# Hybrid encoder step: wide decay rows of the Mixer in three sets of two, loaded one use ahead

## The chip, the cores and the metric

One core of a Trainium2 chip. The metric is the device time of one execution in microseconds. A core has TensorE (PE, matmuls), VectorE (DVE), ScalarE (ACT), GpSimd (POOL) and SyncE (SP). Each engine works through its own instructions in the order in which they were written to it, and an instruction that waits holds those behind it on the same engine. DMA transfers are issued from SP, ACT and POOL; an issue stands in its engine's order like any other instruction.

## The reference

One layer over 512 prompt frames and 64 sample frames (576 columns in the kernel): half a SwiGLU, a Mixer, half a SwiGLU, a norm. The Mixer projects its input once and runs three branches: a Mamba-2 scan in 4 groups of 4 heads (`ssd`), band attention in 8 heads (`attn`), and 4 matrix memories (`ml`). What the change touches are the decays. For the scan, with `cum` the running sum of the log decays over the frames:

```python
cum = jnp.cumsum(dtc * a, axis=1)
seg = cum[:, :, None] - cum[:, None, :]
lmat = jnp.exp(jnp.where(causal, seg, -jnp.inf))
w = cb[..., None] * lmat * dtc[:, None]
y = jnp.einsum('btsgr,bsgrp->btgrp', w, xc)
y = y + jnp.exp(cum)[..., None] * jnp.einsum('btgn,bgrpn->btgrp', cc, h)
wd = jnp.exp(last[:, None] - cum) * dtc
h = jnp.exp(last)[..., None, None] * h + jnp.einsum('bsgr,bsgn,bsgrp->bgrpn', wd, bc, xc)
```

The matrix memories use two such rows for each head, the negated running maximum and `ei`, the factor of the carried state.

## The kernel before

The large matrix products run as a stream of small "products" on PE: a product is twelve matmuls of 128x288 into one PSUM bank (L695). The operands of a product are loaded by DMA, combined by POOL and DVE, and split into a high and a low part by ACT (`ph`, the cast L325) and DVE (`pl`, L326); the casts run five products ahead (`AHEAD`). A finished bank is emptied by ACT (L612, L619) and DVE (L621) before it is used again.

The branches are side jobs beside that stream: `ORDER` puts them as a0 a1 m0 s0 a2 a3 s1 m1 s2 m2 s3 m3 (`a` two heads of attention, `m` one matrix memory, `s` one group of the scan). Each job is a Python generator; `tick()` advances it once for each product, and a `yield n` leaves n products before its next piece. A scheduler then orders all instructions on every engine by a simulated timeline, so an instruction whose inputs the timeline has ready is written earlier than the piece it stands in: work on a decay row moves forward until right behind the load of that row.

The rows of cumulated log decays lie in HBM (`scr_rows`), one for each head. To be used beside a tile of 128 partitions a row is loaded into all partitions. `R1` is a tile of eight rows of 576. Rows 0 and 1 hold the gates `z` of a group. Rows 2 to 7 are two sets of three: `b()` (L181) takes the sets in turn and issues one DMA from ACT's queue that brings two rows (L186, 576 KB). For a matrix memory they are `nmB` and `eiB`. For one half of a group (two heads, `j` 0 or 1) they are the two heads' decays, and the third row of the set takes `ec`: each head's decays again, on 64 partitions each, by two more DMAs of 144 KB (L1281). In `ssd`, the rows of the first half are loaded at the job's start and those of the second half two products later.

What is done with the rows in a half of `ssd`: DVE subtracts them from the token-major log decays for `wd` (L1328, L1329), ACT makes `el` (L1331, L1332) and the exponential of `wd` (L1333). DVE subtracts again, over the whole tile (L1345), and ACT applies Relu (L1348) and Exp (L1351) in place in R1. The product with C·B (L1353) follows, and the matmuls L1388. ACT turns `ec` into its exponential (L1379), DVE multiplies it with the carried part (L1398), and POOL adds it (L1399, L1400). The carried state of the sample frames, `s0` (64 KB), is loaded from ACT's queue when the fifth chunk is reached (L1360) and used by the state update on DVE (L1371) and a matmul (L1397). In `ml`, `wc` (L1168) reads `nmB` on ACT, and `cs` (L1184) reads `eiB` on DVE. `tok_major` (L983) turns k and v with PE (L988, L992) and copies the turned tiles out of PSUM with ACT (L990) and DVE (L994). At the end of the last group the freed rows of R1 take the first rows of the merge (`early`).

Of the kernel before, what the change touches and what calls it, by code (L numbers as in the profile page):

```python
# [32 lines left out]
T = 576  # L33
# [21 lines left out]

ORDER = [(c[0], int(c[1])) for c in "a0 a1 m0 s0 a2 a3 s1 m1 s2 m2 s3 m3".split()]
TC = {"schedule_with_timeline_sim": True}

# [26 lines left out]
class Hybrid:  # L85
    def __init__(self, ctx, tc, I, O):
# [6 lines left out]
        self.steps = None  # L93
        self.b_i = 0
        self.behind = 0
        self.jobs, self.gap, self.side = deque(), 0, iter(())
        nc = self.nc
# [82 lines left out]

    def b(self, step, r0):  # L181


        i = 2 + self.b_i % 2 * 3
        self.b_i += 1
        self.nc.scalar.dma_start(self.R1[:, i:i + 2, :], self.rows(r0, 128, step))  # L186
        return [self.R1[:, i + j, :] for j in range(3)]

# [807 lines left out]
    def attn(self, i, t):  # L996


        nc = self.nc
# [93 lines left out]
        for c in range(4):  # L1093
# [10 lines left out]
            yield 1 + c // 3  # L1104
        PT, _ = turned(Ps[0], 576)
        yield 2
        pv = self.ps("v")
# [25 lines left out]
    def ml(self, h, t):  # L1133
        nc = self.nc
        q, k, v, o = t["q"], t["k"], t["v"], t["o"]
        nmB, eiB, _ = self.b(4, 16 + h)
        C0 = self.unit([128, 130], "c0", 1)
# [5 lines left out]
        self.tok_major(v, v1)  # L1143
        yield 3
        qt = self.t("t")
# [11 lines left out]
        s = self.ps("s")  # L1157
# [9 lines left out]
        for c, (a, n) in enumerate(CH):  # L1167
            nc.scalar.activation(wc[:n, c:c + 1], self.TM[:n, c, 64 + h:65 + h], AF.Exp, bias=nmB[:n, a + n - 1:a + n])  # L1168
        yield 1
        nums = [self.ps("v"), self.ps("x")]  # L1170
        where = [(0, 0), (0, 129), (0, 258), (1, 0), (1, 129)]
        C = None
        for c, (a, n) in enumerate(CH):
# [7 lines left out]
            if c == 0:  # L1181
                i = nc.vector.tensor_copy(C2[:, :129], pc[:, :129])
            else:
                i = nc.vector.scalar_tensor_tensor(C2[:, :129], C[:, :129], eiB[:, a + n - 1:a + n], pc[:, :129],  # L1184
                                                   op0=ALU.mult, op1=ALU.add)
            self.empties(i)
            b, o0 = where[c]
# [8 lines left out]
        r = self.unit([128, 8], "r", 2)  # L1196
# [3 lines left out]
        for c, (a, n) in enumerate(CH):  # L1200
            b, o0 = where[c]
# [3 lines left out]
        for c, (a, n) in enumerate(CH):  # L1205
            b, o0 = where[c]
# [6 lines left out]
        for c, (a, n) in enumerate(CH):  # L1213
            b, o0 = where[c]
            nc.vector.tensor_scalar(hn[:n, c, :], nums[b][:n, o0:o0 + 128], r[:n, c:c + 1], ss[:n, c:c + 1],
                                    op0=ALU.mult, op1=ALU.mult)
        yield 4
        y = o
# [51 lines left out]
    def ssd(self, g, t):  # L1270
        nc = self.nc
        Bf, Cf = t["B"], t["C"]
        rows = []

        at = []

        def load(j):
            at.append(2 + self.b_i % 2 * 3)
            rows.append(self.b(1, 4 * g + 2 * j))
            for r in range(2):  # L1280
                nc.scalar.dma_start(rows[j][2][r * 64:(r + 1) * 64, :], self.rows(4 * g + 2 * j + r, 64))  # L1281
        load(0)

# [4 lines left out]
        yield 2  # L1288
        load(1)
        free = 2 + (self.b_i - 1) % 2 * 3  # L1290
        h4 = lambda ap: ap.rearrange("p c (h e) -> p c h e", e=64)
# [16 lines left out]
        for j in range(2):  # L1308
            x = t[f"x{j}"]
            d0 = 4 * g + 2 * j  # L1310
            *cum, ec = rows[j]

# [21 lines left out]
            for n, cs in ((128, slice(0, 4)), (64, slice(4, 5))):  # L1334
                m = cs.stop - cs.start
                nc.vector.tensor_tensor(h4(xw[:n, cs, :]), h4(xd[:n, cs, :]),
                                        wd[:n, cs, :].unsqueeze(3).broadcast_to([n, m, 2, 64]), op=ALU.mult)
            i = at[j]
            E = self.R1[:, i:i + 2, :]
# [7 lines left out]
            for e in parts:  # L1347
                nc.scalar.activation(e, e, AF.Relu, scale=-1.0)  # L1348
            yield 1
            for e in parts:  # L1350
                nc.scalar.activation(e, e, AF.Exp, scale=-1.0)  # L1351
# [5 lines left out]
            for c, (a, n) in enumerate(CH):  # L1357
                if c == 4:
                    s0 = st()
                    nc.scalar.dma_start(s0, self.I["s0"][:, d0 * 64:d0 * 64 + 128])  # L1360
                    states[4] = s0
# [44 lines left out]
        if g == 3:  # L1406

            self.early = [self.R1[:, i, :] for i in (free, free + 1, free + 2, 0)]
            for i in range(3):
                nc.sync.dma_start(self.early[i], self.ys[i])  # L1410
# [336 lines left out]
```

## Time and profile before

| what | value |
|---|---|
| time, median of 3 runs | 1928.65 us (1926.78 to 1935.07) |
| the profiled execution | 1932.9 us, its span 1931.2 us |
| first SwiGLU | about 0 to 590 us of the span |
| Mixer with the side jobs | about 590 to 1195 us |
| merge of the branches, second SwiGLU, norm | the rest |
| mean granted TensorE clock of the span | 0.99 |

The profile is one execution. Its lists of waits give, for each engine, the line that waited, what released it, the total in us, how many times and the longest. In a timeline row stand the start, the duration, the engine, the line, the operation, the tiles, and in brackets the idle time of that engine ahead of it with the instruction that ended it. A windows row gives for a stretch its length, the busy time of PE, PEld (weight loads), DVE, ACT and POOL with counts, the granted clock, the DMA share and GB/s. Rows of R1 are called `R<-scr_rows` in the DMA list.

### The profile page before, as it was taken

To read this page: it belongs to the slowest core of one execution; us is meant where nothing else is said; L and a number is where in the kernel's file an instruction comes from. 1 tells how busy PE (TensorE), PEld (TensorE's weight loads), DVE (VectorE), ACT (ScalarE), POOL (GpSimd) and SP (SyncE) were. 2 spreads that over 40 slices of the span, in tenths; PEclk is the share of its full clock that TensorE was granted. 3 is DMA by queue.
4 is the path that set the end of the run, shared out by engine and by line. 5 is a ranking of instruction groups with operands and counts; after the bars stand their busy time and mean duration, and the time that the engine had idled before them with its cause. 6 is when DMAs were issued, how large, how long until landed. Compare 5 with 4: busy or idle time off the path is not lost. (4 is left out here: it accounts for less than half of the span.)

```text
span 1931.2 us, 37563 instructions
## 1 busy us (share of the span) xinstructions
PE 1867.1 (97%) x13901; PEld 1816.3 (94%) x13901; DVE 1545.6 (80%) x2763; ACT 1060.0 (55%) x2342; POOL 653.8 (34%) x613
## 2 busy tenths in 40 slices
PE   9899999999999899999898999999999999999998
PEld 9899999999999778888888899999999999999998
DVE  7998898988868768777678786745899898899865
ACT  6564554654534776666565656324565454554544
POOL 3443333433302323422434343440333333343311
PEclk9999999999999999999999999999999999999999
DMA  7357666666742445754656555652446656666631
GB/s 221 104 154 177 155 156 162 155 178 165 180 136 90 139 129 152 214 155 127 180 149 184 148 152 176 217 177 84 113 119 163 168 159 168 163 158 169 153 98 56
DMA packets 129439, 294.69 MB, mean 153 GB/s; under 512 B 14288, under 2 KB 26192, under 8 KB 129256
## 3 DMA queue, kind: packets, MB, share of 16 engines
q1 hardware_dynamic: 99368, 203.42, 32.2%
q0 software_dynamic: 20272, 74.20, 20.7%
q10 hardware_dynamic: 9616, 14.69, 2.6%
q8 instruction: 109, 1.79, 0.4%
q14 instruction: 74, 0.61, 0.1%
HBM read 272.87 MB, written 19.38 MB: 151 GB/s over the span
## 5 line engine op out<-in xcount | busy, mean ns | idle before, releaser
L695 PE MATMUL acc<-TH,ph 128*128 128x288 f32 x3220 | 969.3, 302 | 23.7 <-ACT uv L612 7.7
L695 PE MATMUL acc<-TL,ph 128*128 128x288 f32 x3220 | 957.3, 298 | 1.3 <-DVE TL L326 1.2
L695 PE MATMUL acc<-TH,pl 128*128 128x288 f32 x3220 | 952.0, 296 | 1.7 <-DVE pl L326 1.7
L695 PEld LDWEIGHTS acc<-TH,ph 128*128 128x128 f32 x3220 | 607.9, 189 | 42.2 <-ACT uv L612 9.5
L695 PEld LDWEIGHTS acc<-TH,pl 128*128 128x128 f32 x3220 | 609.5, 190 | 4.1 <-DVE pl L326 2.4
L695 PEld LDWEIGHTS acc<-TL,ph 128*128 128x128 f32 x3220 | 608.9, 189 | 3.6 <-DVE TL L326 2.4
L326 DVE TENSOR_TENSOR pl<-wr,ph 128x512 fp32r<-128x512 f32 x471 | 438.1, 936 | 74.7 <-ACT ph L325 61.7
L325 ACT CAST ph<-wr 128x512 fp32r<-128x512 f32 x471 | 287.6, 618 | 282.4 <-PE acc L695 159.6
L325 ACT CAST ph<-wx 128x512 fp32r<-128x512 f32 x390 | 237.3, 619 | 204.9 <-PE acc L695 102.4
L326 DVE TENSOR_TENSOR pl<-wx,ph 128x512 fp32r<-128x512 f32 x390 | 316.7, 816 | 31.4 <-ACT ph L325 24.7
L551 POOL TENSOR_TENSOR wx<-wx,wr 128x512 f32<-128x512 f32 x160 | 246.7, 1542 | 178.9 <-DVE pl L326 144.2
L539 POOL DMA_DIRECT2D wx<-in_sblk x115 | 101.5, 916 | 514.0 <-DVE pl L326 191.1
L270 PE MATMUL acc<-YH,ph 128*128 128x256 f32 (+1 forms) x768 | 227.4, 298 | 2.5 <-ACT g L619 2.2
L270 PE MATMUL acc<-YL,ph 128*128 128x256 f32 (+1 forms) x768 | 227.6, 297 | 0.6 <-DVE YL L383 0.6
L270 PE MATMUL acc<-YH,pl 128*128 128x256 f32 (+1 forms) x768 | 227.3, 297 | 0.0
L270 PEld LDWEIGHTS acc<-YH,ph 128*128 128x128 f32 x768 | 145.3, 190 | 3.6 <-ACT g L619 2.3
L270 PEld LDWEIGHTS acc<-YL,ph 128*128 128x128 f32 x768 | 145.4, 189 | 1.1 <-DVE YL L383 1.0
L270 PEld LDWEIGHTS acc<-YH,pl 128*128 128x128 f32 x768 | 145.3, 189 | 0.0
L551 POOL TENSOR_TENSOR wy<-wx,wr 128x512 f32<-128x512 f32 x35 | 57.0, 1630 | 144.5 <-DVE pl L326 110.0
L734 DVE SCALAR_TENSOR_TENSOR R<-acc,R 128x288 f32<-128x288 f32 x168 | 75.7, 451 | 19.8 <-PE acc L695 19.0
L325 ACT CAST TH<-g 128x288 fp32r<-128x288 f32 x120 | 51.3, 433 | 51.0 <-POOL g L720 33.2
L720 POOL TENSOR_TENSOR g<-g,P 128x288 f32<-128x288 f32 x56 | 62.9, 1122 | 37.1 <-ACT P L719 37.0
(328 smaller groups left out, 2318.7 us busy)
## 6 DMA issues: line engine op xcount, KB each, us to landing
wr<-in_sblk SPq DMA_DIRECT2D x345, 256.0 KB, 3.6
wx<-in_sblk POOLq DMA_DIRECT2D x119, 512.0 KB, 6.7
wx<-in_sblk SPq DMA_DIRECT2D x111, 512.0 KB, 3.8
wr<-in_wblk SPq DMA_DIRECT2D x126, 256.0 KB, 3.0
R<-scr_rows ACTq DMA_DIRECT2D x12, 576.0 KB, 6.1
gs<-g SPq DMA_DIRECT2D x20, 288.0 KB, 3.9
g<-gs POOLq DMA_DIRECT2D x20, 288.0 KB, 3.6
y<-ys POOLq DMA_DIRECT2D x12, 288.0 KB, 4.9
```

What stands on the lines that cost most here:

```text
L270: last = nc.tensor.matmul(ps[:, :n], wt[:, wsl], xx[:, k0 + k, a:a + n], start=(k == 0 and i == 0), stop=(k == nk - 1 and i == 2))
L325: self.cast = self.nc.scalar.copy(hi, src).ins
L326: self.nc.vector.tensor_tensor(lo, src, hi.bitcast(F32), op=ALU.subtract)
L539: nc.gpsimd.dma_start(x12, src[:, 1:3, :], accum_op=ALU.add)
L551: add = lambda o, one, two: self.nc.gpsimd.tensor_tensor(o, one, two, op=ALU.add)
L695: self.nc.tensor.matmul(ps, wt[:, wsl], xx[:, kk, :], start=(start and kk == 0 and i == 0), stop=(kk == 3 and i == 2), skip_group_check=True)
L720: nc.gpsimd.tensor_tensor(s["g"][:, 1, :], s["g"][:, 1, :], a, op=ALU.mult)
L734: self.nc.vector.scalar_tensor_tensor(o, ps, scale, o, op0=ALU.mult, op1=ALU.add)
```

## The change

- R1's rows 2 to 7 become three sets of two. `decays(n)` issues loads up to the n-th use in the order of a list `ROWS`, and `b()` hands out the oldest loaded set and has the next one loaded. The first is issued at the end of job a1, and from then on each load one use ahead of its use.
- `ec` gets a tile of its own with one buffer, loaded one product after the half has begun.
- `s0` is loaded at the start of each half, with its tile taken there.
- In `ml` the pieces behind the turned tiles come two products sooner (gaps 1, 1, 2, ..., 5 in place of 1, 3, 1, ..., 4; their sum stays).
- `early` takes the first three freed rows of the last group.

```diff
+ROWS = [r for u, i in ORDER for r in {"a": [], "m": [(16 + i, 4)], "s": [(4 * i, 1), (4 * i + 2, 1)]}[u]]
...
-    def b(self, step, r0):
-        i = 2 + self.b_i % 2 * 3
-        self.b_i += 1
-        self.nc.scalar.dma_start(self.R1[:, i:i + 2, :], self.rows(r0, 128, step))
-        return [self.R1[:, i + j, :] for j in range(3)]
+    def decays(self, n):
+        while self.b_i < min(n, len(ROWS)):
+            r0, step = ROWS[self.b_i]
+            i = 2 + self.b_i % 3 * 2
+            self.b_i += 1
+            self.nc.scalar.dma_start(self.R1[:, i:i + 2, :], self.rows(r0, 128, step))
+            self.fetched.append(i)
+
+    def b(self):
+        i = self.fetched.popleft()
+        self.b_n += 1
+        self.decays(self.b_n + 1)
+        return i
...
         PT, _ = turned(Ps[0], 576)
+        if i == 1:
+            self.decays(1)
         yield 2
...
-        nmB, eiB, _ = self.b(4, 16 + h)
+        i = self.b()
+        nmB, eiB = self.R1[:, i, :], self.R1[:, i + 1, :]
...
         self.tok_major(v, v1)
-        yield 3
+        yield 1
...
-        yield 1
+        yield 2
         nums = [self.ps("v"), self.ps("x")]
...
-        yield 4
+        yield 5
         y = o
...
-        def load(j):
-            at.append(2 + self.b_i % 2 * 3)
-            rows.append(self.b(1, 4 * g + 2 * j))
-            for r in range(2):
-                nc.scalar.dma_start(rows[j][2][r * 64:(r + 1) * 64, :], self.rows(4 * g + 2 * j + r, 64))
-        load(0)
+        free = []
...
         yield 2
-        load(1)
-        free = 2 + (self.b_i - 1) % 2 * 3
...
-            *cum, ec = rows[j]
+            i = self.b()
+            free += [i, i + 1]
+            cum = self.R1[:, i, :], self.R1[:, i + 1, :]
+            s0 = st()
+            nc.scalar.dma_start(s0, self.I["s0"][:, d0 * 64:d0 * 64 + 128])
...
             yield 1
+            ec = self.unit([128, T], "ec", 1)
+            for r in range(2):
+                nc.scalar.dma_start(ec[r * 64:(r + 1) * 64, :], self.rows(d0 + r, 64))
             for e in parts:
                 nc.scalar.activation(e, e, AF.Exp, scale=-1.0)
...
                 if c == 4:
-                    s0 = st()
-                    nc.scalar.dma_start(s0, self.I["s0"][:, d0 * 64:d0 * 64 + 128])
                     states[4] = s0
...
-            self.early = [self.R1[:, i, :] for i in (free, free + 1, free + 2, 0)]
+            self.early = [self.R1[:, i, :] for i in (*free[:3], 0)]
```

The counts of instructions are the same on every engine. The orders are alike up to about product 284 and from about product 525 on. Lines of the changed kernel are named by its own numbers: L186 is L188 there, L325 L334, L326 L335, L612 L621, L619 L628, L988 L997, L990 L999, L994 L1003, L1168 L1180, L1281 L1356, L1328 L1333, L1331 L1336, L1345 L1349, L1348 L1352, L1351 L1358, L1360 L1316, L1379 L1384, L1398 L1403. R_60 is R1.

**First place: products 407 to 411, where group 1 of the scan ends and m1 begins with its turns.** The rows here are those of group 2, loaded as soon as a set is free. Before, they are those of its first half, and DVE has this order from the first use of newly loaded rows (`wd`, which waits for the DMA) to the copy of a turned tile that PE needs next; the load itself went out two products earlier.

```order
L1328 TENSOR_TENSOR wd<-R_60,TM 128x4 [waits DMAHW2_49]
L1329 TENSOR_TENSOR wd<-R_60,TM 64x1
L1328 TENSOR_TENSOR wd<-R_60,TM 128x4
L1329 TENSOR_TENSOR wd<-R_60,TM 64x1
L1345 TENSOR_TENSOR R_60<-R_60,TM 128x2x512 [waits DVE_49,Activation_49]
L1345 TENSOR_TENSOR R_60<-R_60,TM 64x2x64 [waits DVE_49,Activation_49]
L337 TENSOR_TENSOR sumsq<-sumsq,sq 128x256 [waits Activation_49]
L326 TENSOR_TENSOR pl<-wr,ph 128x512 [waits PE_49]
L326 TENSOR_TENSOR pl<-wy,ph 128x512 [waits PE_49,Pool_49]
L994 COPY t<-ps_x 64x128 [waits PE_49]
```

Now the first half's rows have been loaded and used earlier, and the load issued at product 407 is that of the second half. ACT has, from this load on:

```order
L188 DMA R_60<-scr_rows 128x1152 [waits PE_49]
L334 CAST ph<-wx 128x512 [waits DMASW3_49,PE_49]
L632 ACTIVATE g<-g 128x288 [waits DVE_49]
L334 CAST ph<-wr 128x512 [waits DMAHW4_49,PE_49]
L632 ACTIVATE g<-g 128x288 [waits DVE_49]
L1336 ACTIVATE el<-R_60 128x4 [waits DMAHW0_49]
L1337 ACTIVATE el<-R_60 128x1
L1336 ACTIVATE el<-R_60 128x4
L1337 ACTIVATE el<-R_60 128x1
L334 CAST ph<-wr 128x512 [waits DMAHW5_49,PE_49]
L1356 DMA ec<-scr_rows 64x576 [waits Pool_49]
L999 COPY t<-ps_x 128x512 [waits PE_49]
```

The load and the first use of its rows stay two products apart, but they belong to the next half. The turns of k (L997, L1001) now stand at products 407 to 409, ahead of or beside this use, and behind it on ACT stand a cast (L334), the first issue of `ec` (L1356), which waits for POOL, and the copy L999 of a turned tile. The same stands at products 456 to 459 with the rows of group 3.

**Second place: products 421 to 426, at the end of m1.** Before, ACT issues the rows of the second half of group 2 here and, four products later, reads them with `el`; this is the piece from the load on (`junk` are the squares of a norm, `uv` and `P` banks on their way out of PSUM).

```order
L186 DMA R_60<-scr_rows 128x1152 [waits DMAHW2_49,DVE_49]
L1138 DMA c_13639<-in_mc 128x129
L325 CAST ph<-wr 128x512 [waits DMAHW1_49,PE_49]
L612 ACTIVATE uv<-acc 128x288 [waits PE_49]
L1208 ACTIVATE junk,ss<-ps_v,r 128x128 [waits DVE_49,Activation_49]
L1208 ACTIVATE junk,ss<-ps_v,r 128x128 [waits Activation_49]
L325 CAST ph<-wy 128x512 [waits PE_49,Pool_49]
L612 ACTIVATE uv<-acc 128x288 [waits PE_49]
L1241 COPY P<-zero 128x3 [waits DVE_49,Activation_49]
L1242 COPY P<-cst 128x3
```

Now the load issued at product 421 is that of m2's rows, and ACT reads them with `wc` at product 423:

```order
L1220 ACTIVATE junk,ss<-ps_v,r 128x128 [waits Activation_49]
L1220 ACTIVATE junk,ss<-ps_x,r 128x128 [waits Activation_49]
L334 CAST ph<-wr 128x512 [waits DMAHW5_49,PE_49]
L1220 ACTIVATE junk,ss<-ps_x,r 64x128 [waits Activation_49]
L1180 ACTIVATE wc<-TM,R_60 128x1 [waits DMAHW1_49]
L1180 ACTIVATE wc<-TM,R_60 128x1 x3
L1180 ACTIVATE wc<-TM,R_60 64x1
L334 CAST ph<-wr 128x512 [waits DMAHW2_49,PE_49]
L1263 COPY co<-P 128x3 [waits DVE_49]
L1264 COPY co<-P 128x3 [waits DVE_49]
L334 CAST ph<-wy 128x512 [waits PE_49,Pool_49]
L628 ACTIVATE P<-acc 128x288 [waits PE_49]
```

The first use of the rows of group 2's second half has moved ahead to the first place, and `wc` of the next matrix memory has moved in, ahead of the casts and of the bank evacuation L628 (L619 before). At products 470 to 472 the same stands with m3's rows.

**Third place: products 301 to 305, in the attention of jobs a2 and a3, for group 0 of the scan.** Before, ACT has Relu and Exp of one half here, among casts and the pieces of the softmax (L1026, L1039):

```order
L1348 ACTIVATE R_60<-R_60 128x2x512 [waits DVE_49]
L1348 ACTIVATE R_60<-R_60 64x2x64 [waits DVE_49]
L623 ACTIVATE g<-g 128x288 [waits DVE_49]
L325 CAST ph<-wr 128x512 [waits DMAHW2_49,PE_49]
L1039 COPY Q<-ps_x 128x512 [waits PE_49]
L1026 ACTIVATE P<-P,sm 128x576 [waits DVE_49,Activation_49]
L186 DMA R_60<-scr_rows 128x2x576 [waits DMAHW0_49,PE_49]
L325 CAST ph<-wr 128x512 [waits PE_49]
L1351 ACTIVATE R_60<-R_60 128x2x512 [waits Activation_49]
L1351 ACTIVATE R_60<-R_60 64x2x64 [waits Activation_49]
L325 CAST ph<-wy 128x512 [waits PE_49,Pool_49]
```

Now both halves stand there:

```order
L1338 ACTIVATE wd<-wd 128x10
L334 CAST ph<-wx 128x512 [waits DMASW4_49,PE_49]
L1352 ACTIVATE R_60<-R_60 128x2x512 [waits DVE_49]
L1352 ACTIVATE R_60<-R_60 64x2x64 [waits DVE_49]
L1048 COPY Q<-ps_x 128x512 [waits PE_49]
L188 DMA R_60<-scr_rows 128x2x576 [waits DMAHW1_49,PE_49]
L1352 ACTIVATE R_60<-R_60 128x2x512 [waits DVE_49]
L1352 ACTIVATE R_60<-R_60 64x2x64 [waits DVE_49]
L632 ACTIVATE g<-g 128x288 [waits DVE_49]
L1358 ACTIVATE R_60<-R_60 128x2x512 [waits Activation_49]
L1358 ACTIVATE R_60<-R_60 64x2x64 [waits Activation_49]
L334 CAST ph<-wr 128x512 [waits PE_49] x2
```

The second half's Relu and Exp have moved in from products after 320; the exponential of `ec` for the second half has moved out.

More of the change, by code (lines that the diff above doesn't have):

```diff
@@ L93, in __init__ @@
         self.steps = None
-        self.b_i = 0
+        self.b_i, self.b_n, self.fetched = 0, 0, deque()
         self.behind = 0
@@ L1272, in ssd @@
         Bf, Cf = t["B"], t["C"]
-        rows = []
-        at = []
-        def load(j):
-            at.append(2 + self.b_i % 2 * 3)
-            rows.append(self.b(1, 4 * g + 2 * j))
-            for r in range(2):
-                nc.scalar.dma_start(rows[j][2][r * 64:(r + 1) * 64, :], self.rows(4 * g + 2 * j + r, 64))
-        load(0)
+        free = []
         last = nc.scalar.activation(self.R1[:, 0, :], self.R1[:, 0, :], AF.Silu)
@@ L1337, in ssd @@
                                         wd[:n, cs, :].unsqueeze(3).broadcast_to([n, m, 2, 64]), op=ALU.mult)
-            i = at[j]
             E = self.R1[:, i:i + 2, :]
```

## The prediction

> **What bounds the kernel now.** I read the busy shares first, then what TensorE (PE) waited for inside the Mixer (600 to 1260 us of the trace; the orders of both programs differ only there), then the waits of ACT and DVE, then the gaps of PE one by one.
>
> ```profile
> PE 1867.1 (97%) x13901; PEld 1816.3 (94%) x13901; DVE 1545.6 (80%) x2763; ACT 1060.0 (55%) x2342; POOL 653.8 (34%) x613
> 600.00:1260.00 660.00, 616.73 (x4617) 575.26 (x4616) 496.53 (x1042) 406.21 (x1002) 238.04 (x248) 0.98 0.57 160
> ```
>
> PE is busy 97% of the span; in the Mixer it is busy 616.73 of 660 us. No work is removed by the change, so all that can be won is idle time of PE in the Mixer, 43 us, and time lost there to the granted clock (0.98 in the mean).
>
> ```profile
> PE ps_x L988 <- DVE t L994: 10.5, 2, 5.3
> PE acc L695 <- ACT uv L612: 7.7, 9, 1.1
> PE ps_x L1397 <- DMA st<-in_s: 2.1, 1, 2.1
> ACT el L1331 <- DMA R<-scr_rows: 14.3, 7, 3.2
> ACT wc L1168 <- DMA R<-scr_rows: 2.5, 3, 1.2
> DVE wd L1328 <- DMA R<-scr_rows: 15.3, 6, 3.0
> DVE st L1371 <- DMA st<-in_s: 7.4, 2, 3.8
> R<-scr_rows ACTq DMA_DIRECT2D x12, 576.0 KB, 6.1
> R<-scr_rows ACTq DMA_DIRECT2D x16, 144.0 KB, 3.5
> L186 ACTq DMA_DIRECT2D R<-scr_rows x12: 327/352/517, 671.1 to 1142.3; - x12
> DMA to landing us min/median/max: 4.1/6.1/6.8
> ```
>
> ACT and DVE together stand some 40 us in wait for decay rows or the state s0. A pair of rows needs 6.1 us from issue to landing (4.1 to 6.8). A product, twelve matmuls, takes some 1.66 us (29 matmuls in the 4 us from 748.00 below), so that is nearly four products. But PE is five casts ahead of them, so only part of this reaches PE. The gaps of PE that begin behind such a wait are these:
>
> ```profile
> 747.96 0.40 PE L695 MATMUL acc<-TH,ph 128*128 128x288 f32 x1 [1.94 <-DVE g L621]
> 790.85 0.68 PE L1397 MATMUL ps_x<-g,st 128*128 128x64 f32 x2 [2.12 <-DMA st<-in_s]
> 949.77 1.11 PE L988 MATMUL ps_x<-ident,g 128*128 128x128 f32 x4 [5.17 <-DVE t L994]
> 983.76 0.37 PE L695 MATMUL acc<-TH,ph 128*128 128x288 f32 x1 [0.36 <-DVE P L621]
> 988.46 0.40 PE L695 MATMUL acc<-TH,pl 128*128 128x288 f32 x1 [0.94 <-DVE pl L326]
> 990.85 0.97 PE L1221 MATMUL ps_x<-ident,Q 128*128 128x128 f32 x3 [0.81 <-DVE Q L1215]
> 1060.88 0.69 PE L988 MATMUL ps_x<-ident,g 128*128 128x128 f32 x2 [5.31 <-DVE t L994]
> 1094.03 0.40 PE L695 MATMUL acc<-TH,ph 128*128 128x288 f32 x1 [0.32 <-ACT P L619]
> 1096.55 0.37 PE L695 MATMUL acc<-TH,ph 128*128 128x288 f32 x1 [0.66 <-DVE P L621]
> 1099.18 0.40 PE L695 MATMUL acc<-TH,pl 128*128 128x288 f32 x1 [0.53 <-DVE pl L326]
> 1101.57 0.33 PE L1221 MATMUL ps_x<-ident,Q 128*128 128x128 f32 x1 [0.80 <-DVE Q L1215]
> ```
>
> They sum to 1.94 + 2.12 + 5.17 + 5.31 + 2.11 + 2.31 = 19.0 us. After three of them the clock is at half:
>
> ```profile
> 748.00:752.00 4.00, 4.00 (x29) 3.75 (x29) 4.00 (x10) 3.97 (x7) 0.85 (x1) 1.00 0.87 219
> 790.90:794.30 3.40, 3.40 (x14) 3.27 (x14) 3.37 (x8) 0.49 (x4) 2.19 (x2) 0.50 0.16 51
> 949.80:954.70 4.90, 4.90 (x21) 4.90 (x22) 1.75 (x4) 4.60 (x11) 4.68 (x3) 0.50 0.18 54
> 1060.90:1063.90 3.00, 3.00 (x13) 3.00 (x14) 0.93 (x2) 3.00 (x8) 3.00 (x2) 0.50 0.30 93
> ```
>
> The seventh figure is the granted clock. Half a clock over 3.4, 4.9 and 3.0 us costs 1.7, 2.5 and 1.5 us, 5.7 in all. The gap of 1.94 us was followed by a full clock, that of 2.12 us by half a clock: the border lies near 2 us here. So 24.7 us hang on late rows and late states. That is the most that this change can win.
>
> **The change part by part.** (1) Third set, loads one use ahead. The orders, set against the products of before, say when each load is issued and when it is first used. The 1.94 us gap is that of group 0's second half, whose rows had to wait for a set to come free; they are loaded at product 298 now (part 5), and at product 322 stands the load of group 1's first half, used some ten products later: **-1.9**. For group 1's second half and the first halves of groups 2 and 3 the distance is three products or more, so nothing is left of the wait but the far end of the landing times.
>
> (2) s0 loaded at the start of each half instead of at its last chunk. It is issued some five products ahead of its use, with 64 KB, whose like took under four us (DVE's longest wait for it, 3.8). The gap of 2.12 us and its half clock go: **-3.8**. What takes its place is nothing on PE: DVE only keeps its order.
>
> (3) The second halves of groups 2 and 3 (orders above, first place). The load is issued a few instructions earlier than the load that stood there before, but the scheduler pulls el and wd up to two products behind it. So the wait stays:
>
> ```profile
> 938.81 0.33 ACTq L186 DMA_DIRECT2D R<-scr_rows  x1
> 944.32 0.27 PE L992 MATMUL ps_x<-ident,g 128*64 128x128 f32 x1
> 944.54 0.21 ACT L1331 ACTIVATE el<-R 128x4 f32<-128x4 f32 x1 [2.82 <-DMA R<-scr_rows]
> 944.54 1.49 DVE L1328 TENSOR_TENSOR wd<-R,TM 128x4 f32<-128x4 f32 x1 [2.68 <-DMA R<-scr_rows]
> 946.28 1.42 DVE L1345 TENSOR_TENSOR R<-R,TM 128x1024 f32<-128x1024 f32 x2
> 949.44 0.27 DVE L994 COPY t<-ps_x 64x128 f32<-64x128 f32 x1
> L325 ACT CAST ph<-wr 128x512 fp32r<-128x512 f32 x471 | 287.6, 618 | 282.4 <-PE acc L695 159.6
> 952.86 0.58 ACT L990 COPY t<-ps_x 128x512 f32<-128x512 f32 x1
> ```
>
> Before, PE stopped at 944.6 and needed DVE's copy L994 (949.44), which stands behind wd, the subtraction L1345 and two casts. After, the k transposes are already done, and the next wait of PE is for ACT's copy L999, which stands behind el, one cast and an issue: landing 944.5, el to 944.95, cast 0.6 (L325), copy 0.6 (L990 before), so PE goes on at some 946.8 with the issue between them. The idle time falls from 5.17 to about 2.2 us. The gap nearest to 2.2 us is that of 2.12, so I leave a half clock of 3.4 us (1.7) in: 7.7 becomes 3.9, **-3.8**; the same at 1060.88, 6.8 becomes 3.9: **-2.9**. Bounds: nothing (L999 is held as long as L994 was) to -7.7 and -6.8 (landing in time).
>
> By the Trainium skill, "TensorE: Matmul & The Clock Gate", section "Why this matters for your kernels", only gaps of TensorE above some 3 us bring the clock down; by that rule both of these would keep a full clock and the sum below would be 3.4 us lower. The trace disagrees: 2.12 us was enough at 790.85.
>
> (4) Rows of the matrix memories (second place). m2's and m3's rows are now issued at products 421 and 470, and wc, which reads them on ACT, comes two products later: 3.2 us against 6.1, so ACT stands some 3 us, with bank evacuations L628 and L621 and the casts behind it. PE needs the bank of L628 at product 425; after wc (0.6) and two casts (1.1) it is some 2.5 to 3 us late. Before, the waits of group 2's and 3's second half stood here and cost PE 2.11 and 2.31 (983.76 to 990.85, 1094.03 to 1101.57). Those go. I put it at **0**; bounds -4.4 (ACT's wait hidden by the five casts ahead) and +5.0 (3 us of idle and half a clock, 4.7, less 2.2, at each of two places). m1's rows at 343.25 are used at 345.67: a wait like those of wc before, 1.2 at the longest, with no slack in the bank: **+1**, from 0 to 2.
>
> (5) Group 0. Both halves' wd, el, subtraction, Relu and Exp now fall into the attention's last part (products 299 to 305; third place), where ACT is full:
>
> ```profile
> 668.00:686.00 18.00, 16.29 (x126) 13.78 (x126) 10.66 (x35) 17.34 (x45) 4.57 (x8) 1.00 0.61 166
> L1348 ACT ACTIVATE R<-R 128x1024 f32<-128x1024 f32 (+1 forms) x16 | 10.3, 674 | 0.6 <-DVE R L1345 0.6
> L1351 ACT ACTIVATE R<-R 128x1024 f32<-128x1024 f32 (+1 forms) x16 | 10.1, 678 | 0.0
> ```
>
> ACT is busy 17.34 of 18 us. Two more Relu (0.67 each) and up to two more Exp come in ahead, less an ec Exp moved out: some 2 us, and a wait of 1 to 2.5 us of DVE for the second half's rows (issued one product ahead of use). The attention chains (scores, softmax, turn) run over ACT and DVE, so most of it reaches PE; the stretch after it is lighter. I take **+1.5**, bounds 0 and 4.
>
> (6) Own ec tile: its loads of 144 KB (3.5) are issued a product later and used some products on. In one buffer they wait on ACT for POOL's last use of the group before (as L1281 did for its row): 0, up to 1 in all. Matrix memory two products sooner: the sum of its products is unchanged; 0.
>
> Sum: -1.9 - 3.8 - 3.8 - 2.9 + 0 + 1 + 1.5 = **-9.9 us**. Against the profiled execution (1932.9, span 1931.2) that is 1923.0; the median of the three runs shown is 4.25 us below this execution, and set against it the time is **1918.8**. A measurement of this kernel tells about 0.5%, 9.6 us, from no change: the forecast lies on that border.
>
> **The rivals.** (a) The loads come in time everywhere: were a pair of rows down in about 3.5 us, as the 144 KB loads are, the waits at 409, 423, 458 and 472 would all but go, and the 24.7 us with them, less the 1.5 of the attention: 1905.5. For it: the queue of ACT carries less at those places. Against: all twelve of before took 4.1 to 6.8. By the Trainium skill, "DMA: Bandwidth & Descriptors", section "Anatomy of one DMA — SWDGE (gpsimd) path", a transfer takes about 2.0 us and its bytes at 436 GB/s, an estimate of 3.4 us for 576 KB; by that rule this rival is the result. The trace disagrees, with 6.1.
>
> (b) The waits only change places: the scheduler puts each consumer right behind its load again, at 299, 345, 409, 423, 458 and 472. If (3) gives nothing, since L999 is held by the ec issue in front of it (which waits for POOL), then -1.9 - 3.8 + 2.5 = -3.2: 1925.5. For it: the six places are in the order. Against: what PE waits for at 409 no longer stands behind 3 us of DVE work.
>
> (c) Slower: a wait of ACT ahead of a bank evacuation. Before, wd and el waited mostly with DVE's casts behind them, five ahead; now wc (345, 423, 472) and el with the copy L999 and uv (409, 458) hold ACT, whose evacuations have no slack. If each of the five places costs 5.2 as at 949.77, and a half clock of 1.7 behind it, that is 34.5 + 1.5 - 24.7 = +11.3: 1940. It decides from (24.7 - 1.5) / 5 = 4.6 us a place on. Against: the waits are bound by the landing at some 3 us.
>
> **How the numbers follow.** Forecast (waits partly kept) 0.50, (a) 0.18, (b) 0.20, (c) 0.12. The forecast spreads by its bounds over 1911 to 1927, half of it faster by over 0.5%; (a) is all faster by over 0.5%; (b) lies within 0.5%; (c) is a range from 1930 to 1945, two thirds above 1938. Faster 0.18 + 0.25 = 0.43, slower 0.08, same 0.49. The range from 1904 to 1931 leaves out most of (c) and the far end of (a).
>
> **What would show it.** Right: no PE gap with an s0 load as releaser; DVE's wait for in_s0 gone; the gap of 1.94 gone; at products 410 and 459 gaps of 2 to 2.5 us with ACT's copy L999 as releaser; ACT's wait for rows moved to wc, 3 us twice, with PE gaps behind evacuations L621 or L628 there. Wrong: if ACT's waits for rows fall under 5 us in all, (a); if the gaps at 410 and 459 stay near 5, (b); if PE's waits for ACT evacuations grow past 15 us, (c). If new idle time shows in the attention between 670 and 700 of over 4 us, (5) was priced too low.

## The result, and the profile after

| | median | ratio to before, 95% interval |
|---|---|---|
| before, 11 runs | 1931.94 us | |
| changed kernel, 11 runs | 1924.52 us (1918.1 to 1926.82) | 0.996 [0.9948, 0.9972] |

The change makes the kernel 7.4 us faster, 0.4%: 9.9 us less was forecast. (The forecast of 1918.8 us was set against a median of 1928.65 us of three runs; that of the eleven runs before is 3.3 us higher.) The span of the profiled execution fell by 7.2 us, from 1931.2 to 1924.0.

First the page's busy times of the changed kernel, and its windows row of the Mixer stretch, with columns as before:

```profile
PE 1865.2 (97%) x13901; PEld 1815.5 (94%) x13901; DVE 1532.9 (80%) x2763; ACT 1058.1 (55%) x2342; POOL 654.1 (34%) x613
```

```profile
600.00:1260.00 660.00, 621.65 (x4656) 582.12 (x4656) 490.29 (x1041) 405.62 (x1002) 244.62 (x256) 0.98 0.59 164
```

In the same 660 us PE is busy 4.9 us longer than before (616.73); the granted clock is 0.98 still. Its waits in the Mixer, and those of ACT and DVE for rows, from the lists of waits:

```profile
PE acc L704 <- ACT uv L621: 16.4, 12, 3.6
PE acc L704 <- ACT P L628: 5.7, 3, 3.3
ACT ph L334 <- DMA R<-scr_rows: 11.6, 2, 6.5
ACT ec L1384 <- DMA ec<-scr_rows: 10.2, 5, 3.3
ACT wc L1180 <- DMA R<-scr_rows: 7.2, 4, 3.5
ACT L1384 <- DMA ec<-scr_rows: 3.9, 1, 3.9
ACT el L1336 <- DMA R<-scr_rows: 2.7, 2, 1.3
DVE wd L1333 <- DMA R<-scr_rows: 4.3, 5, 1.7
```

What was to go is gone: el waits 2.7 us instead of 14.3, wd 4.3 instead of 15.3, and the rows for the turns (10.5) and for s0 (2.1) are no longer in PE's list. `wc` waits 7.2 us instead of 2.5. And there is a wait that was not there: 14.1 us of ACT for `ec` (10.2 ahead of the exponential, 3.9 in a row that names no tile). PE's waits for banks that ACT empties grew from 7.7 to 16.4 (`uv`) and from 0.7 to 5.7 (`P`); the second of these stood before as

```profile
PE acc L695 <- ACT P L619: 0.7, 2, 0.4
```

The gaps of PE over 1.3 us between products 320 and 505:

```profile
782.14 0.43 PE L704 MATMUL acc<-TH,ph 128*128 128x288 f32 x1 [1.39 <-ACT uv L621]
927.78 0.40 PE L704 MATMUL acc<-TH,ph 128*128 128x288 f32 x1 [2.98 <-ACT uv L621]
972.12 0.40 PE L704 MATMUL acc<-TH,ph 128*128 128x288 f32 x1 [1.51 <-ACT P L628]
1035.17 0.61 PE L704 MATMUL acc<-TH,ph 128*128 128x288 f32 x1 [1.81 <-ACT uv L621]
1081.12 0.40 PE L704 MATMUL acc<-TH,ph 128*128 128x288 f32 x1 [3.25 <-ACT P L628]
1144.48 0.61 PE L704 MATMUL acc<-TH,ph 128*128 128x288 f32 x1 [3.56 <-ACT uv L621]
```

They stand at products 340, 403, 424, 452, 473 and 501. To see the whole balance I set the start of each product in the trace of after against that of before. A column is what a stretch gained (less than zero) or lost, worked out as the difference of these differences at its ends; it holds idle time, clock, and work of the side jobs that PE does in another stretch than before:

| products | what lies there | after less before, us |
|---|---|---|
| 0 to 296 | same order in both programs | -2.5 |
| 296 to 322 | attention, rows of group 0 | +0.9 |
| 322 to 334 | the 1.94 us gap of before | -6.1 |
| 334 to 340 | second half of group 0, `ec` | +3.3 |
| 340 to 400 | s0's gap of before; group 1's rows | -2.2 |
| 400 to 406 | second half of group 1, `ec` | +4.4 |
| 406 to 412 | the 5.17 us gap of before | -7.4 |
| 412 to 446 | wc of m2 | -0.6 |
| 446 to 454 | second half of group 2, `ec` | +3.8 |
| 454 to 462 | the 5.31 us gap of before | -6.3 |
| 462 to 496 | wc of m3 | +0.9 |
| 496 to 503 | second half of group 3, `ec` | +4.7 |
| 503 to 526 | end of the stream | -0.8 |

The first row is not the change's: the orders are alike there, and such an offset differs from one execution to the next. The rest is -5.4 us: some 23 us won, 18 given back, 16.2 of these at the four places of `ec`. Not all of that is waiting. From 322 to 334 PE has 225 matmuls before and 201 after, from 334 to 340 95 and 111: work moved from one stretch into the other, and PE's idle time alone fell by 3.6 us in the first and grew by 1.6 in the second. Idle time and half clocks at the four places of `ec` together grew by 15.4 us.

This is what happens at the second of the four. The rows are the timeline of ACT, with the engine's issues (ACTq), and one of POOL:

```profile
917.04 0.60 POOL L1405 TENSOR_TENSOR g<-g,ec 128x64 f32<-128x64 f32 x1
917.67 0.46 ACTq L1356 DMA_DIRECT2D ec<-scr_rows  x1
918.25 0.62 ACT L334 CAST ph<-wx 128x512 fp32r<-128x512 f32 x1 [5.08 <-DMA R<-scr_rows]
918.27 0.73 ACTq L1356 DMA_DIRECT2D ec<-scr_rows  x1
922.63 0.24 ACT L1371 COPY st<-ps_s 128x128 f32<-128x128 f32 x1
926.13 0.68 ACT L1384 ACTIVATE ec<-ec 128x576 f32<-128x576 f32 x1 [3.25 <-DMA ec<-scr_rows]
926.82 0.60 ACT L334 CAST ph<-wy 128x512 fp32r<-128x512 f32 x1
927.33 0.70 ACT L621 ACTIVATE uv<-acc 128x288 f32<-128x288 f32 x2
```

The issue of `ec` waits until POOL has used the one buffer for the last time (L1405 ends at 917.64). ACT does nothing for 5.08 us ahead of the cast behind it; the list gives this wait to rows of R1, but the cast starts right behind the issue. The second load is issued at 918.27, and its exponential, written two products behind, starts at 926.13: 3.25 us of waiting ACT. The evacuation L621 stands behind that exponential, and PE stands 2.98 us for its bank, to 927.78.

### The profile page after: what moved, and what is told of

It reads as the page before. It is cut to its first block, busy times and chain, and to the rows that moved or that the text cites. A ratio compares the mean times of both kernels' runs of the same rounds, so it can differ in the third digit from the quotient of the medians.

```text
span 1924.0 us, 37528 instructions
## 1 busy us (share of the span) xinstructions
PE 1865.2 (97%) x13901; PEld 1815.5 (94%) x13901; DVE 1532.9 (80%) x2763; ACT 1058.1 (55%) x2342; POOL 654.1 (34%) x613
## 5 line engine op out<-in xcount | busy, mean ns | idle before, releaser
L704 PE MATMUL acc<-TH,ph 128*128 128x288 f32 x3220 | 970.3, 302 | 34.2 <-ACT uv L621 16.4
L335 DVE TENSOR_TENSOR pl<-wr,ph 128x512 fp32r<-128x512 f32 x471 | 430.3, 919 | 70.3 <-ACT ph L334 59.0
L334 ACT CAST ph<-wr 128x512 fp32r<-128x512 f32 x471 | 287.2, 618 | 263.8 <-PE acc L704 142.5
L334 ACT CAST ph<-wx 128x512 fp32r<-128x512 f32 x390 | 237.1, 619 | 213.5 <-POOL wx L560 101.4
L335 DVE TENSOR_TENSOR pl<-wx,ph 128x512 fp32r<-128x512 f32 x390 | 312.3, 804 | 46.3 <-ACT ph L334 39.8
L560 POOL TENSOR_TENSOR wy<-wx,wr 128x512 f32<-128x512 f32 x35 | 49.9, 1425 | 134.0 <-DVE pl L335 112.6
L334 ACT CAST TH<-g 128x288 fp32r<-128x288 f32 x120 | 51.4, 433 | 50.4 <-POOL g L729 32.9
L335 DVE TENSOR_TENSOR pl<-wy,ph 128x512 fp32r<-128x512 f32 x70 | 54.4, 777 | 26.9 <-ACT ph L334 16.7
```

The costliest lines, as they stand in the source:

```text
L334: self.cast = self.nc.scalar.copy(hi, src).ins
L335: self.nc.vector.tensor_tensor(lo, src, hi.bitcast(F32), op=ALU.subtract)
L560: add = lambda o, one, two: self.nc.gpsimd.tensor_tensor(o, one, two, op=ALU.add)
L704: self.nc.tensor.matmul(ps, wt[:, wsl], xx[:, kk, :], start=(start and kk == 0 and i == 0), stop=(kk == 3 and i == 2), skip_group_check=True)
```

## The experiments

The trace left three readings of why ACT waits for `ec`. **Theory A**: one buffer for `ec` loads it too late. **Theory B**: the scheduler writes the exponential of `ec` right behind its load, in front of the evacuations, however early the load. **Theory C**: the issue itself, which waits for POOL, holds ACT. All ratios are to the kernel before, timed on the same chip; the changed kernel is at 0.996.

### Two buffers for ec (e1_two_ec)

```diff
-            ec = self.unit([128, T], "ec", 1)
+            ec = self.unit([128, T - 128], "ec", 2)
...
-                nc.scalar.dma_start(ec[r * 64:(r + 1) * 64, :], self.rows(d0 + r, 64))
+                nc.scalar.dma_start(ec[r * 64:(r + 1) * 64, :], self.rows(d0 + r, 64)[:, 128:])
```

> ec in two buffers of 448 columns (room for them from one buffer less of junk and cs). In the changed kernel PE stands at products 340, 403, 452 and 501 (1.39, 2.98, 1.81, 3.56 us, 9.7 in all, each with a half clock of 3.4 us behind it), each time for a bank that ACT empties late, because the exponential of ec stands in front of it and waits for its load. Theory A (the single buffer makes the load late): with two buffers the load goes out a whole half earlier, the four gaps go, 10 to 15 us less than the changed kernel, ratio to before 0.988 to 0.991. Theory B (the scheduler writes the exponential right behind its load, however early that is): the loads of the next half stand where those of this one stood, the exponential again two to three products behind, and the gaps at 340, 403 and 452 stay; only the one at 501 goes (no load left to follow), ratio 0.993 to 0.996.

Measured: 1924.54 us, 0.9963 [0.9948, 0.9978]: the time of the changed kernel. Theory A's time falls. Theory B has the time right, and the traces show its order: the loads are issued at products 337.5 and 399.5 in the changed kernel and at 338.0 and 400.0 here, now for the next half, with the exponential two products behind again (339.8 and 402.6), still ahead of the evacuation L621. But the gaps speak for A in part. Those at 403, 452 and 501 are not in this trace, of which B had let only the last go, and ACT's wait for `ec` is down, by the list of its waits in the Mixer:

```profile
ACT ec L1384 <- DMA ec<-scr_rows: 4.4, 4, 2.0
```

(112 KB land in 4.1 us, against 5.9 for 144 KB in the changed kernel). At 340 PE stands 2.75 us in two pieces, at 347 2.03, at 424 2.68. Set against the trace of before as in the table, the stretches of `ec` behind 400 cost nothing in this trace (+0.8, -0.2 and -0.5 us, where the changed kernel has +4.4, +3.8 and +4.7). The attention costs 3.6 instead of 0.9, and most other stretches 0.7 to 2.4 us more. Why the time came back there is not shown: gaps that go at these places are not by themselves time won.

### The exponential of ec tied to its use (e2_exp_late)

```diff
-            nc.scalar.activation(ec, ec, AF.Exp)
+            e = nc.scalar.activation(ec, ec, AF.Exp)
+            self.tc.add_manual_dep(e.ins, i.ins.name, READY, reason="last state")
```

`i` is the last state update of the half on DVE, so the exponential can't be written before it. Loads and buffer stay.

> As the changed kernel, with one buffer and its loads where they are, but the exponential of ec is tied behind the last state update of its half on DVE, so it can't be written ahead of the evacuations at 340, 403, 452 and 501. Theory B: the four gaps and their half clocks go, 10 to 15 us less than the changed kernel, ratio 0.988 to 0.991. Theory A (a late load is late wherever it is used): the wait goes to the multiplication L1404 or its matmul, the time stays, ratio 0.995 to 0.997. Theory C (what holds ACT is the issue of ec itself, which waits for POOL; 5.1 us of idle ACT ahead of product 401): the gaps shrink by less than half, ratio 0.993 to 0.995.

Measured: 1916.6 us, 0.9929 [0.9916, 0.9942], below the interval of the changed kernel. Theory B holds, at some 6 us instead of 10 to 15. ACT's wait for the loads of `ec` is gone from its list, and so are the gaps at 403, 452 and 501; the one at 340 is 1.09 us, behind a state copy. The lists of waits in the Mixer (PE, then ACT), and from PE's timeline the gap at 424, show what is left:

```profile
PE acc L704 <- ACT uv L621: 8.6, 10, 1.4
PE acc L704 <- ACT P L628: 8.4, 4, 3.5
ACT wc L1180 <- DMA R<-scr_rows: 9.1, 3, 3.7
```

```profile
973.07 0.61 PE L704 MATMUL acc<-TH,ph 128*128 128x288 f32 x1 [3.49 <-ACT P L628]
```

`wc` waits 9.1 us in front of `P` L628. That is part of the missing size: the gap of 1.51 us at product 424 is 3.49 here. So is the attention, which costs 3.5 us in this trace.

### ec loaded from POOL's queue (e3_ec_pool_queue, e4_pool_and_late)

```diff
-                nc.scalar.dma_start(ec[r * 64:(r + 1) * 64, :], self.rows(d0 + r, 64))
+                nc.gpsimd.dma_start(ec[r * 64:(r + 1) * 64, :], self.rows(d0 + r, 64))
```

> As the changed kernel, but the two loads of ec are issued from POOL, behind its own last use of the buffer, so ACT no longer waits for POOL with an issue. Theory C: the gaps at 340, 403, 452 and 501 go or fall under 1 us, ratio 0.989 to 0.992. Theory B: the exponential still stands in front of the evacuations and waits for its load; what is gone is only the casts' delay, and the gaps keep 2 us or more at 403 and 501, ratio 0.994 to 0.997.

Measured: 1926.1 us, 0.998 [0.9968, 0.9992]. Theory C falls as the cause of the loss: with the issue off ACT's queue nothing is won, and ACT still waits 10.9 us for `ec`, by its list in the Mixer:

```profile
ACT ec L1384 <- DMA ec<-scr_rows: 7.2, 5, 2.5
ACT L1384 <- DMA ec<-scr_rows: 3.7, 1, 3.7
```

The gap at 501 is 3.08 us and that at 452 1.63; the one at 340 is down to 0.73. The one at 403 is down to 1.04, which B had put at 2 or more.

Both edits together:

> Both edits: ec loaded from POOL's queue, its exponential tied behind the last state update. Theories B and C together say no gap of PE over 1 us at 340, 403, 452 and 501 and the lowest time of the four, ratio 0.987 to 0.990; theory A says the multiplication waits in their place, ratio 0.995 to 0.997.

Measured: 1919.35 us, 0.9937 [0.9924, 0.995]: the time of the tied exponential alone, not lower, and not the 0.987 to 0.990 of B and C together. The gaps at 403, 452 and 501 are gone again; theory A's 0.995 to 0.997 lies outside the interval but for its edge. With the exponential tied, the queue makes no difference that can be told.

### Parts of the change undone (e5_two_sets, e6_s0_late, e7_ml_gaps, e10_no_lookahead)

Two sets of two in place of three:

```diff
-            i = 2 + self.b_i % 3 * 2
+            i = 2 + self.b_i % 2 * 2
```

> As the changed kernel, but two sets of two in place of three; ec, s0 and the gaps of the matrix memories stay as changed. Theory D (the third set is what took the gaps of 1.94, 5.17 and 5.31 us away): without it the rows of a half are loaded right ahead of their use again, wd and el wait, and gaps of 2 us at product 325 and 3 to 5 us at 409 and 458 return with their half clocks, while the wait of wc at 423 and 472 goes: 8 to 12 us more than the changed kernel, ratio to before 1.000 to 1.003. Theory E (the own ec tile alone did it, since it lets the load go when E is used up): as the changed kernel, 0.995 to 0.997.

In this kernel the rows that the merge loads early take the place of m3's decays, so m3's part of the output and what follows from it is not the reference's; no work is left out. Measured: 1936.29 us, 1.0029 [1.0017, 1.0041], 0.7% or 13 us over the changed kernel, in the ratio that theory D gave. The waits of the first users are back, as the list of DVE's waits and PE's timeline show,

```profile
DVE wd L1333 <- DMA R<-scr_rows: 12.7, 5, 2.9
```

```profile
749.87 0.40 PE L704 MATMUL acc<-TH,ph 128*128 128x288 f32 x1 [1.58 <-DVE g L630]
```

and with them the gap at product 325. But the 5 us gaps at 410 and 459 are not: 1.25 and 1.06 us. So the third set accounts for the first of the three old gaps only; what took the other two is the rest of the new order. Between the two profiled executions lie 9.7 us, 5.7 of them from product 322 to 334 and 2.3 in the attention.

s0 loaded at its chunk, and the matrix memory's gaps as before, each by itself:

> As the changed kernel, but s0 loaded when its chunk is reached, as before. The prediction's part 2: the gap of 2.12 us behind DMA st returns at product 343, with a half clock: 2 to 4 us more than the changed kernel, ratio 0.997 to 0.998. Rival: the scheduler lifts this load to the moment its buffer is free in any case, and the waits for ec stand in front of it, so nothing changes: 0.995 to 0.9965.

> As the changed kernel, but the gaps of the matrix memory as before (1, 3, 1, ..., 4). The prediction's part 6: no difference within 2 us, ratio 0.995 to 0.997, with the wait of wc at 424 and 473 half a product later. Rival: the sooner matrix memory is what took the gaps of L1221 (0.81 and 0.80 us) and of the bank evacuations at 426 to 432 away, and 3 us or more come back: 0.9975 or more.

Measured: 1921.39 us, 0.9954 [0.9939, 0.9969], and 1923.69 us, 0.9959 [0.9944, 0.9974]. Neither can be told from the changed kernel. The s0 row is the prediction's miss: its gap does not return. In the trace the load of this place is issued at product 340.7 and used at 343.4; before, it was issued at 339.5 and used at 340.9. It is the use that comes later in the new order, not the load that comes much sooner.

But that run is not a test of s0 alone. Its order has the exponential of `ec` behind the evacuation L621 at product 403, with nothing tied, as ACT's timeline shows:

```profile
927.50 0.71 ACT L621 ACTIVATE uv<-acc 128x288 f32<-128x288 f32 x2
931.75 0.68 ACT L1384 ACTIVATE ec<-ec 128x576 f32<-128x576 f32 x1
```

The gaps at 340, 403, 452 and 501 are all gone in this trace, as theory B would have it, and the four stretches cost 0.3 us in all. Against that stand a gap of 2.84 us at 347 and stretches that gain less than in the changed kernel; four timed runs don't tell whether s0 late costs what this order wins. The matrix memory's row is as forecast.

The look-ahead in the text undone, three sets kept:

```diff
+        self.decays(self.b_n + 1)
         i = self.fetched.popleft()
         self.b_n += 1
-        self.decays(self.b_n + 1)
```

> As the changed kernel, but each pair of rows is loaded where the program text uses it, not one use ahead; three sets stay. The scheduler lifts a load to the moment its set is free, so this order differs from that of the changed kernel in a few dozen rows near product 298 only. Theory: the look-ahead in the text does nothing, the third set does it, same as the changed kernel, ratio 0.995 to 0.997. Rival: the order near 298 matters (group 0's first load comes later), 2 us or more lost in the attention, 0.9975 or more.

Measured: 1923.32 us, 0.9968 [0.9954, 0.9982]: not to be told from the changed kernel, nor from the rival's 0.9975. From product 320 on the loads of rows are issued where the changed kernel has them, to a tenth of a product: the scheduler issues a load when its set is free, wherever the text has it. Nearer to 298 the rival shows in the trace. The attention costs 9.2 us against before, where the changed kernel's cost 0.9, with ACT standing for the rows of m0:

```profile
690.15 0.29 ACT L1178 ACTIVATE wc<-TM,R 128x1 f32<-128x1 f32 x1 [4.34 <-DMA R<-scr_rows]
```

That load took 10.05 us to land, 6.57 in the changed kernel. Whether the order or this one execution made it slow is open; the median shows no loss of that size.

### wc, and all first users, tied (e8_exp_and_wc_late, e9_all_tied)

```diff
-            nc.scalar.activation(wc[:n, c:c + 1], ...
+            i = nc.scalar.activation(wc[:n, c:c + 1], ...
+            self.tc.add_manual_dep(i.ins, scored.ins.name, READY, reason="scores")
```

> As e2_exp_late, and in addition wc of a matrix memory is tied behind DVE's scores of the same head, so it is not written right behind the load of its rows. The prediction's part 4 (wc waits some 3 us on ACT in front of bank evacuation L628): the gaps at 424 and 473, 3.49 and 3.00 us in e2_exp_late with half clocks behind them, fall under 1 us; 6 to 10 us less than e2_exp_late, ratio 0.987 to 0.990. Rival: ACT is late there for another reason (the casts and norms of the matrix memory), and the gaps stay: 0.992 to 0.994.

Measured: 1915.8 us, 0.9912 [0.9897, 0.9928]. The gaps at 424 and 473 fall from 3.49 and 3.00 to 1.46 and 1.28 us, and ACT's wait of `wc` for rows is gone. DVE's L1162, which reads the same rows, now waits 5.7 us for m3's. In time it is 0.17% below the tied exponential alone, with intervals that overlap: the mechanism shows in the trace, the forecast of 6 to 10 us doesn't hold, and the rival's 0.992 is not ruled out. New gaps stand behind DVE (`R` L630, 4.2 us in three).

Last, `wd` and `el` too are tied, behind the turned x of their half:

```diff
+                with self.tc.issue_after(turned.ins):
+                    nc.vector.tensor_tensor(wd[:, 0:4, r], last, ...
...
+                e = nc.scalar.activation(el[:, 0:4, r], last, AF.Exp)
+                self.tc.add_manual_dep(e.ins, turned.ins.name, READY, reason="x turned")
```

> As e8_exp_and_wc_late, and in addition the first users of a half's rows (wd on DVE, el on ACT) are tied behind the turned x of the same half, so that nothing that reads a row stands right behind its load any more; every load has five products or more. Theory F (what is left is still the eager reading: Relu and Exp of both halves of group 0 in the attention, el and wd at 409 and 458): the waits for rows go to zero on ACT and DVE, the attention from product 298 to 312 gets 2 to 4 us shorter, 2 to 6 us less than e8_exp_and_wc_late, ratio to before 0.988 to 0.990. Rival G (the early work also filled idle time of ACT and DVE; put back to its place it piles up at each half's start, ahead of evacuations): gaps of PE of 1 us and more at products 331, 338, 394 to 403 and 443 to 452, and the time is that of e8_exp_and_wc_late or up to 6 us more, ratio 0.991 to 0.995.

Measured: 1910.18 us, 0.9907 [0.9889, 0.9925], the lowest of all, some 0.5% below the changed kernel, whose interval it clears. No wait for rows is left in the lists of ACT and DVE. In the list of PE's waits in the Mixer the lines of ACT's bank evacuations in the product stream are now short, and the windows row of the Mixer has PE busier:

```profile
PE acc L704 <- ACT uv L621: 4.4, 5, 1.1
PE acc L704 <- ACT g L628: 3.5, 6, 0.8
```

```profile
600.00:1260.00 660.00, 633.19 (x4782) 592.45 (x4781) 515.89 (x1062) 416.04 (x1016) 263.80 (x260) 0.99 0.59 170
```

PE is busy 633.19 of the 660 us, 11.5 more than in the changed kernel. From product 296 to 312 this trace gains 1.7 us on that of before, e8_exp_and_wc_late nothing: a little less than theory F's 2 to 4. Rival G's piles do not show: 0.8 us each at 340, 403 and 452. That it is faster than the version with `ec` and `wc` tied is not settled by the times, and the interval reaches into the ranges of F and G both.

A good part of the gain is clock. Between products 296 and 526 PE idles 24.6 us and is busy at half clock for 6.0; in the changed kernel it was 35.7 and 25.5. In the timed runs the mean granted clock is 0.992 to 0.996, against 0.989 to 0.993 in those of the changed kernel.

## Why the prediction was right, and where not

The direction and the size came out (9.9 us forecast, 7.4 measured), but the sum is near by luck: its terms missed in both ways, (6) alone by more than the whole sum.

- **(1) The third set, -1.9.** Right in kind, too small: PE's idle time from product 322 to 334 fell by 3.6 us (the other 2.5 of the stretch are work that moved behind it). With the wait went two more gaps behind it, at product 326; the larger stood before as

```profile
753.55 1.16 PE L1298 MATMUL ps_s<-g 128*128 128x128 f32 x8 [1.49 <-ACT g L1287]
```

  Two sets bring the wait back. Of the look-ahead in the text no worth can be told from the times.
- **(2) s0, -3.8.** The gap went, but it stays away with s0 loaded late too, where the use is later by 2.5 products. So the term belongs at least as much to the rest of the new order as to this edit. I had also read the price too low, "under four us" from a wait of DVE; the loads themselves took up to 5.0 before (least, median and most from issue to landing):

```profile
DMA to landing us min/median/max: 1.9/3.1/5.0
```
- **(3) Products 410 and 459, -6.7.** The gaps and their half clocks went whole, 7.7 and 6.8 us, the bound that I had given for a landing in time. I had read the issue from the order as a few instructions earlier; in the trace it stands at product 405.8, where before's stood at 406.9. From the timelines of ACT and PE of the changed kernel:

```profile
934.54 0.33 ACTq L188 DMA_DIRECT2D R<-scr_rows  x1
940.16 0.21 ACT L1336 ACTIVATE el<-R 128x4 f32<-128x4 f32 x1 [1.33 <-DMA R<-scr_rows]
941.07 0.57 ACT L999 COPY t<-ps_x 128x512 f32<-128x512 f32 x1
942.42 0.60 PE L997 MATMUL ps_x<-ident,g 128*128 128x128 f32 x4
```

  The landing took 5.6 us, as priced; el waited 1.33, and the copy L999 was done ahead of PE's need, so no idle time was left in place of my 2.2. Which edit set this order is open. With the third set, s0, the gaps of the matrix memories or the look-ahead undone, each by itself, no gap over 1.25 us comes back there; the tile of its own for `ec` is the edit that was never undone.
- **(4) wc, 0.** Right in the sum: -0.6 and +0.9. The gaps of 1.51 and 3.25 us behind `P` L628 took the place of those of before, by the mechanism forecast, though not at the distance: in the trace the loads are issued at products 419.2 and 468.2, four ahead of `wc`, and `wc` waited 1.75 and 3.50 us where I had some 3 each (m3's rows took 8.63 us to land). Tied to its use, `wc` no longer waits on ACT. Of the +1 for m1, `wc` waited 1.52 us, and no gap of PE over 0.8 us follows it.
- **(5) Attention, +1.5.** Inside its bounds: +0.9 in this trace, 0 to 3.6 in those of the variants, but for 9.2 without the look-ahead and -1.7 with all readers tied.
- **(6) The own ec tile, 0 to 1.** This is the step that failed. I wrote that its loads in one buffer wait for POOL as L1281 did, priced them at 3.5 us (5.9 in the changed kernel), and left out the exponential that the scheduler writes behind them, and what is queued behind that. Measured +16.2 us at four places of the trace, 15.4 of them idle time and half clock. It is theory B: tying that one instruction gives some 6 us back by the times of the runs; neither another buffer nor another queue does. What stays open is why the buffer takes three of the four gaps away and wins no time, so 16.2 is what stands at these places and not what the step costs.

So the rival that I called (c), a wait of ACT ahead of a bank evacuation, was real, and the sign that I had named for it was met: PE's waits for ACT's evacuations came to 22.1 us (16.4 and 5.7), past 15. It stood mostly at other places than the five I listed, and the larger gains at (1) and (3) paid for it. Rival (a) set the fit of the Trainium skill, "DMA: Bandwidth & Descriptors", against these loads; its section gives that fit for transfers issued from GpSimd, and the loads of rows go out from ACT. Here 144 KB issued from GpSimd took 4.9 us (e3_ec_pool_queue).

## What to carry to other kernels

Where a scheduler lifts each instruction to the moment its inputs are ready by its own timeline, look less at where a load stands in the text than at what the first reader of its data stands in front of: on an engine that works in order, a reader lifted behind a slow load holds everything behind it (3.25 us of ACT and 2.98 of PE at product 403). Price with each load the instruction that reads it first, by the measured landing time, and name what is queued behind. Tying that reader to its real use takes no memory, and here it was worth more than a further buffer (0.9929 against 0.9963).

## What the runs showed of the hardware

The clock did not go by the length of a gap. These are windows of the changed kernel, behind the gaps of 1.39, 2.98 and 3.25 us (the seventh figure is the granted clock):

```profile
782.40:785.80 3.40, 3.40 (x16) 3.40 (x16) 1.25 (x3) 1.42 (x3) 1.28 (x1) 0.50 0.06 17
929.20:932.50 3.30, 3.30 (x16) 3.30 (x15) 2.37 (x5) 2.78 (x6) 1.66 (x2) 0.50 0.07 20
1081.20:1084.50 3.30, 3.30 (x25) 3.30 (x26) 3.30 (x11) 3.23 (x9) 2.26 (x2) 1.00 0.28 84
```

A gap of 1.39 us was followed by half a clock, one of 3.25 us by a full one, so my border near 2 us was wrong as well.

The Trainium skill, "TensorE: Matmul & The Clock Gate", section "What's actually happening", has TensorE's activity watched in a window of some 3.4 us that runs freely; a gap's place in it would then count, not its length alone. The runs agree. In all twelve traces the stretches of half clock between the first product and the end of the merge are 3.41 us long or a multiple of it (up to 17.07), and within a trace they start a whole number of 3.413 us apart, to 0.01 of that step. Laid on this grid from 95 us to 1.9 ms, the windows at full clock part by PE's busy share: all 31 under 0.47 were followed by half a clock, none over 0.66, and 26 of the 89 between. The gap of 1.39 us fell whole, with smaller ones, into one window, where PE was busy for 0.48; that of 3.25 us was split over two, with 0.57 and 0.48. All three lie in the range where either may follow: the longer gap left no emptier window than the shorter one. So a gap is priced by the idle time of its window, not by its length. Where the grid lies differs from one execution to the next.

The loads of `ec`, 144 KB, took as long as those of 576 KB, by the list of DMA issues in the Mixer of the changed kernel (the last figure is the median from issue to landing in us):

```profile
R<-scr_rows ACTq DMA_DIRECT2D x12, 576.0 KB, 5.8
ec<-scr_rows ACTq DMA_DIRECT2D x16, 144.0 KB, 5.9
```

Before, loads of that size into R1 took 3.5 us. In the variants with 144 KB the medians lie from 4.1 to 5.6. Why is not settled. And the gaps of one program differ between executions: the offset of 0 to 3 us that the profiles have to each other by product 282, where all orders are alike, is as large as several of the terms here, so only differences that the timed intervals or several places bear out are called shown.
